# Holding ScalarE to the source's order while the first three QKV chunks are issued

## The chip, the cores and the metric

The kernel runs on one NeuronCore of a Trainium2 chip. The metric is the device time of one execution in microseconds (us). Below, PE is TensorE (matmuls), DVE is VectorE, ACT is ScalarE, POOL is GpSimd, and SP is SyncE, whose queue issues the large DMA loads. "Landing" of a load is the moment its data is in SBUF.

## The reference

A decoder trunk of two layers on 256 positions of width 2048, all in float32. Layer 0 has sliding-window attention (32 query heads, 4 key/value heads of 64), layer 1 a gated linear recurrence; each is followed by a squared-ReLU MLP of width 8192. Every half-layer is normalised and modulated by vectors computed from a conditioning vector. What matters here is the start of layer 0:

```python
cond = jax.nn.silu(c)
mod = cond @ mod_w[i] + mod_b[i]                       # 6 vectors of 2048 per layer
sh1, sc1, g1, sh2, sc2, g2 = jnp.split(mod, N_MOD, axis=-1)
h = modulate(rms_norm(x, norm_mix[i]), sh1, sc1)       # h * (1 + sc1) + sh1
proj = h @ w_in                                        # QKV: 2048 -> 2048 + 256 + 256
q = rms_norm(q, q_gain); k = rms_norm(k, k_gain)       # per head
out = softmax(banded q k^T with ALiBi and a sink) @ v
x = x + g1 * (out @ w_out)
h = modulate(rms_norm(x, norm_mlp[i]), sh2, sc2); a = relu(h @ w1); x = x + g2 * ((a * a) @ w2)
```

All weights are read once, 594 MB in all.

## The kernel before, in words

Weights come in pieces of 128 x 2048 float32 (1024 KB). A piece is loaded by SP into one of five `raw` buffers (`load_to`, L208 to L214). A weight piece then becomes two matmul operands: ACT rounds each half of it to `wh` (L250), DVE subtracts to get the remainder `wl` (L251). There are five half-size buffers for `wh` and five for `wl`, and a piece takes two of each. A product is three matmuls, weight-high times data-high, weight-high times data-low, and weight-low times data-high.

The pieces come in one list, `seq`, and are loaded in that order. In the QKV stage there are three kinds. "w" are weight pieces. "g" are modulation weights that PE multiplies with the conditioning vector straight from `raw` (`gemv`, 4 matmuls named `mm<-raw,cst`); after four of them a row is copied by ACT (L267), turned by PE (`gt`), and reduced by DVE into `mods` (L273). "m" are modulation weights that DVE multiplies and sums in one instruction (L233). A `raw` buffer is free again when its piece has been used: for w at the end of `wl`, for g at the end of the gemv, for m at the end of the DVE instruction.

The QKV product is split along its inner dimension into four chunks of 512 (chunk 0 to 3, the loop variable `s_`, L862), so that it can begin before all modulation vectors are known. A chunk has five w pieces (below w20 is the first piece of chunk 2), and each piece gives two results of 128 x 512 in PSUM, "halves" of the piece: 24 matmuls each. In chunks 0 to 2 a g and an m follow each of the first four pieces in `seq`, which makes 13 loads per chunk. ACT copies each half out of PSUM. In chunk 0 the copy goes straight to its place (`first_part`, L851, tiles `o`), in chunks 1 and 2 to a scratch tile `w` (`add_part`, L846) from which POOL adds it (L847). In chunk 3 DVE adds the last part, and what follows is the per-head normalisation: ACT squares (L676, L703), PE sums (`ssq`) and turns (`sst`), DVE takes the reciprocal root (L651, L132 to L138), widens it (L662), PE turns it back (`rbk`), DVE multiplies (L725), and the first attention pair (`S` matmuls) can begin. Before a chunk, its four input tiles `h` are made by DVE and ACT from `mods` (`make_h`: `ht` L547, `h` high part L551 on ACT, low part L552 on DVE).

In the source, `ahead(LAG - 1)` behind each piece's products prepares one piece more than the one that comes next: the `wh` casts of piece n+1 are written ahead of the products and copies of piece n.

The order in which each engine's instructions stand is not the source's. A scheduler in the recording layer (`TileContext`) orders them when the program is built. Instructions of one engine that don't depend on each other can change places. Two front ends hold PE to an order: `Queue` wraps an engine, remembers the name of its last instruction, and, where `pin` is true, adds to each new one a dependency on the one before, which costs no semaphore and no instruction. `pe` records without pinning, `pep` pins, and both share one `last`.

Of the kernel before, what the change touches and what calls it, by code (L numbers as in the profile page):

```python
# [41 lines left out]
class Queue:  # L42
# [5 lines left out]
    def __getattr__(self, name):  # L48
        fn = getattr(self.engine, name)

        def call(*args, **kw):
            r = fn(*args, **kw)  # L52
            if self.pin and self.last:
                self.tc.add_manual_dep(
                    r.ins, self.last[-1],
                    mybir.DependencyInfo(mybir.DependencyClass.NoSync, mybir.DependencyReason.DATA),
                    reason="issue order")
            self.last[:] = [r.ins.name]
            return r
        return call  # L60
# [2 lines left out]
@with_exitstack  # L63
def trunk(ctx, tc, a, out):
    nc = tc.nc
    dve, act, sp, pool_q = nc.vector, nc.scalar, nc.sync, nc.gpsimd
    last = []
    pe, pep = Queue(tc, nc.tensor, last, False), Queue(tc, nc.tensor, last, True)

# [239 lines left out]
    def ahead(extra, must=True):  # L309
        w = min(st["w"] + extra, len(wpos) - 1)  # L310
        while st["prep"] <= wpos[w]:
            if seq[st["prep"]][0] != "w" and st["hold"] and not must:
                break
            prep_one()
# [109 lines left out]
    def mm_quarter(op, k0, natural, evacs):  # L424
        key = st["w"]
        ahead(0)
        for j in range(2):
            ps = mmtile()
            wh, wl = W[key][j]
            if natural[j]:  # L430
                for k in range(4):
                    v_step(ps, wh, wl, k, op[k0 + k], k == 0, k == 3)
                    if k % 2 == 1:
                        hook()
            else:
                for u in range(2):
                    for k in range(4):
                        c = slice((4 * u + k) * P, (4 * u + k + 1) * P)
                        three(ps[:, u * T:(u + 1) * T], wh[:, c], wl[:, c], op[k0 + k], k == 0, k == 3)
                    hook()  # L440
            evacs[j](ps)
        W.pop(key)
        st["w"] += 1
        ahead(LAG - 1, False)
# [166 lines left out]
    with tc.tile_pool(name="attn", bufs=2) as ap:  # L611
# [207 lines left out]
        def step():  # L819
            s_ = steps[0]  # L820
            steps[0] += 1
            hook()
            if DT + DV <= s_ < 16 + DT + DV:
                pair_v(s_ - DT - DV)
            if DT <= s_ < 16 + DT:
                pair_t(s_ - DT)
            if s_ < 16:
                while s_ // 2 not in rq or not kdone:
                    hook()
                pair(s_)  # L830
            if 1 <= s_ < 17:
                pair_n(s_ - 1)
            if s_ >= 9:
                for _ in range(2):
                    if wo["k"] <= min(KB - 1, s_ - 5):
                        wo_step()
            hook()
            for _ in range(2):
                if seq[st["prep"]][0] != "w":
                    prep_one()  # L840
            ahead(0, False)
# [11 lines left out]
        def done_part(p):  # L853
# [6 lines left out]
                    evac_q(p - 2, ps, parts[p])  # L860
            return f
        for s_, fin_part in enumerate((first_part, add_part, add_part, done_part)):  # L862
            feed.need(4 * s_ + 4)
            st["hold"] = s_ == 3
            ahead(LAG - 1, False)
            for e in range(5):
                mm_quarter(H, 4 * s_, (False, e == 0), (fin_part(2 * e), fin_part(2 * e + 1)))
                feed.poll()
                for _ in range(SE if s_ == 3 and e > EE else 0):
                    step()  # L870
                ahead(LAG - 1, False)
# [483 lines left out]
```

## Time and profile before

| | us |
|---|---|
| three runs | 2344.27, 2355.24, 2355.31 |
| the profiled execution, its own time | 2348.51 |
| its span, first to last instruction | 2346.7 |
| PE busy | 2269.6 (97%) |
| DVE busy | 1788.2 (76%) |
| ACT busy | 1163.1 (50%) |
| POOL busy | 100.7 (4%) |

The profiled execution's time is 1.8 us more than its span. The page cuts the span into 40 slices of 58.7 us; PE is at nine tenths or more in all but the first five, which hold the start, the QKV stage and the attention. The mean granted TensorE clock is 0.99. In the tables below a row of a windows view has, for each stretch, its length, PE busy with the number of records, the granted clock, the busy share of the DMA engines and their GB/s (with all engines shown, PE, PEld, DVE, ACT, POOL come in that order). In a timeline a row is start, duration, engine, line, operation, tiles, and in brackets how long the engine had been idle and what ended that.

### The profile page before, as it was taken

The numbers are of one execution on the slowest core, as the hardware profiler recorded it, in microseconds if no ns is written. First come the engines' busy times: TensorE is split into PE (matmuls) and PEld (weight loads), VectorE is DVE, ScalarE is ACT, GpSimd is POOL, SyncE is SP. The second block draws the span as 40 slices with busy tenths as digits, with TensorE's granted clock in tenths as the row PEclk, the third lists the DMA queues.
The fourth block names the chain that finished last, engine by engine and source line by source line (L and its number), as shares of the span: only waits on it lengthen the run. The fifth ranks groups of instructions, "written<-read, shape, count | busy, mean of one in ns | idle before, by whom it ended". The sixth has DMA issues, their size and how long they took to land.

```text
span 2346.7 us, 37064 instructions
## 1 busy us (share of the span) xinstructions
PE 2269.6 (97%) x14690; PEld 1992.0 (85%) x14690; DVE 1788.2 (76%) x2908; ACT 1163.1 (50%) x1962; POOL 100.7 (4%) x94
## 2 busy tenths in 40 slices
PE   5887899999999999999999999999999999999999
PEld 3775579998888888888888898899888888888888
DVE  5668679975888898897998888767865766665665
ACT  3344454544444444455666666655544444444443
POOL 0133530000000000000000000000000000000000
PEclk8999999999999999999999999999999999999999
DMA  9886799756898899985577777645666666655552
GB/s 361 310 305 257 272 335 341 253 195 215 323 336 323 327 333 324 334 317 187 196 284 267 259 267 268 214 164 180 231 233 231 236 227 239 207 189 186 191 194 94
DMA packets 84638, 598.80 MB, mean 255 GB/s; under 512 B 9457, under 2 KB 11505, under 8 KB 12273
## 3 DMA queue, kind: packets, MB, share of 16 engines
q1 hardware_dynamic: 81936, 593.81, 70.3%
q8 instruction: 115, 1.88, 0.3%
q10 hardware_dynamic: 2304, 2.10, 0.3%
q0 software_dynamic: 224, 0.52, 0.1%
q14 instruction: 59, 0.48, 0.1%
HBM read 594.04 MB, written 2.10 MB: 254 GB/s over the span
## 4 chain that ended last, share of the span: by engine, by line
PE 92%; DVE 4%; ACT 2%; DMA 1%; issue 1%; POOL 0%; ACTq 0%; SPq 0%; DVEq 0%; POOLq 0%
PE mm L52 89%; ACT wh L250 1%; DVE raw L233 1%; PE A L52 1%; DVE wl L251 1%; PE on L52 0%; PE S L52 0%; POOL h L771 0%; DVE asm L751 0%; DMA raw<-in_aoutk_dram 0%; DMA raw<-in_mod_w_dram 0%; PE cb L52 0%; PE pt L52 0%; DVE h L552 0%; PE pv L52 0%
## 5 line engine op out<-in xcount | busy, mean ns | idle before, releaser
L251 DVE TENSOR_TENSOR wl<-raw,wh 128x1024 fp32r<-128x1024 f32 x744 | 909.3, 1226 | 429.7 <-ACT wh L250 427.9
L250 ACT CAST wh<-raw 128x1024 fp32r<-128x1024 f32 x744 | 778.4, 1050 | 850.9 <-PE mm L52 773.2
L52 PE MATMUL mm<-h,wh 128*128 128x512 f32 (+2 forms) x3728 | 1155.4, 368 | 35.1 <-ACT wh L250 34.6
L52 PE MATMUL mm<-h,wl 128*128 128x256 f32 (+1 forms) x3232 | 908.9, 282 | 1.5 <-DVE wl L251 1.4
L52 PE MATMUL mm<-o,wh 128*128 128x512 f32 (+2 forms) x3120 | 860.4, 346 | 0.2 <-ACT h L759 0.2
L52 PEld LDWEIGHTS mm<-h,wh 128*128 128x128 f32 x3728 | 671.5, 190 | 161.9 <-ACT wh L250 39.0
L52 PE MATMUL mm<-o,wl 128*128 128x256 f32 (+1 forms) x2432 | 679.2, 280 | 0.0
L52 PEld LDWEIGHTS mm<-h,wl 128*128 128x128 f32 x3232 | 612.2, 190 | 11.1 <-issue 3.4
L52 PEld LDWEIGHTS mm<-o,wh 128*128 128x128 f32 x3120 | 539.9, 189 | 82.3 <-issue 2.5
L52 PEld LDWEIGHTS mm<-o,wl 128*128 128x128 f32 x2432 | 457.9, 188 | 0.7 <-issue 0.3
L233 DVE CUSTOM_DVE_ANT_0 raw<-raw,cond 128x2048 f32<-128x2048 f32 x160 | 365.7, 2286 | 9.5 <-DMA raw<-in_mod_w_dram 9.3
L52 PE MATMUL mm<-wh,h 128*128 128x256 f32 x576 | 105.9, 283 | 4.2 <-DVE h L552 2.7
L52 PEld LDWEIGHTS mm<-wh,h 128*128 128x128 f32 x576 | 88.8, 188 | 8.0 <-DVE h L552 3.2
L52 PE MATMUL mm<-wl,h 128*128 128x256 f32 x288 | 81.0, 281 | 0.0
L472 ACT COPY w<-mm 128x256 f32<-128x256 f32 x186 | 68.1, 366 | 0.0
L771 POOL TENSOR_SCALAR h<-h,asm 128x128 f32<-128x128 f32 x64 | 64.6, 1027 | 69.7 <-DVE asm L754 21.1
L476 ACT CAST h<-w 128x256 fp32r<-128x256 f32 x125 | 49.8, 403 | 23.9 <-DVE w L967 23.0
L52 PEld LDWEIGHTS mm<-wl,h 128*128 128x128 f32 x288 | 54.3, 188 | 0.5 <-issue 0.4
L967 DVE SCALAR_TENSOR_TENSOR w<-w 128x256 f32<-128x256 f32 x125 | 52.0, 421 | 2.2
L477 DVE TENSOR_TENSOR h<-w,h 128x256 fp32r<-128x256 f32 x125 | 51.5, 417 | 0.0
L473 DVE TENSOR_TENSOR w<-mm,w 128x256 f32<-128x256 f32 x109 | 45.6, 418 | 0.4 <-ACT w L472 0.2
L988 DVE TENSOR_TENSOR acc<-mm,acc 128x256 f32<-128x256 f32 x96 | 40.5, 422 | 6.3 <-PE mm L52 3.8
(203 smaller groups left out, 1134.6 us busy)
## 6 DMA issues: line engine op xcount, KB each, us to landing
raw<-in_mod_w_dram SPq DMA_DIRECT2D x160, 1024.0 KB, 5.5
raw<-in_mlp_dram SPq DMA_DIRECT2D x128, 1024.0 KB, 4.9
raw<-in_hin_dram SPq DMA_DIRECT2D x64, 1024.0 KB, 5.0
raw<-in_mlp1b_dram SPq DMA_DIRECT2D x64, 1024.0 KB, 4.8
raw<-in_mlp1a_dram SPq DMA_DIRECT2D x48, 1024.0 KB, 5.2
raw<-in_mod_g_dram SPq DMA_DIRECT2D x32, 1024.0 KB, 6.1
raw<-in_ainq_dram SPq DMA_DIRECT2D x20, 1024.0 KB, 6.8
raw<-in_m1h_dram SPq DMA_DIRECT2D x16, 1024.0 KB, 5.1
```

Of the source, the lines that this page charges most:

```text
L52: r = fn(*args, **kw)
L233: dve.tensor_tensor_reduce(out=r, in0=r, in1=cond, scale=1.0, scalar=0.0, op0=ALU.mult, op1=ALU.add, accum_out=mods[:, e[1], e[2]:e[2] + 1])
L250: act.copy(out=wh, in_=part)
L251: dve.tensor_tensor(out=wl, in0=part, in1=wh.bitcast(F32), op=ALU.subtract)
L472: act.copy(out=t, in_=ps[:, T:])
L473: dve.tensor_tensor(out=out_t, in0=ps[:, :T], in1=t, op=ALU.add)
L476: act.copy(out=opt[:, :T], in_=src_t)
L477: dve.tensor_tensor(out=opt[:, T:2 * T], in0=src_t, in1=opt[:, :T].bitcast(F32), op=ALU.subtract)
L771: pool_q.tensor_scalar(out=Ls[hh][:, cut[b]], in0=Ls[hh][:, cut[b]], scalar1=ri[:, i:i + 1], scalar2=None, op0=ALU.mult)
L967: dve.scalar_tensor_tensor(out=t, in0=t, scalar=0.0, in1=t, op0=ALU.max, op1=ALU.mult)
L988: dve.tensor_tensor(out=acc[n], in0=ps[:, :T], in1=acc[n], op=ALU.add)
```

## The change

ACT gets a front end of its own (`act = Queue(tc, nc.scalar, [], False)`). It pins while the loop issues chunks 0 to 2 (`s_ < 3`), and not before or after. PE, DVE, POOL and SP are recorded as before. No instruction is added or taken away, and no buffer, size or wait is set by hand. The edit from `self.last` to `self.last[:1]` has the same truth value. Because all ACT calls now go through the wrapper, ACT's instructions bear the line L52 of the wrapper instead of their own, and the other lines behind L65 move by one, behind L863 by two.

```diff
         def call(*args, **kw):
             r = fn(*args, **kw)
-            if self.pin and self.last:
+            if self.pin and self.last[:1]:
                 self.tc.add_manual_dep(
...
     nc = tc.nc
-    dve, act, sp, pool_q = nc.vector, nc.scalar, nc.sync, nc.gpsimd
+    dve, sp, pool_q = nc.vector, nc.sync, nc.gpsimd
+    act = Queue(tc, nc.scalar, [], False)
     last = []
     pe, pep = Queue(tc, nc.tensor, last, False), Queue(tc, nc.tensor, last, True)
...
         for s_, fin_part in enumerate((first_part, add_part, add_part, done_part)):
+            act.pin = s_ < 3
             feed.need(4 * s_ + 4)
```

What it moves, in three places. First ACT in chunk 1. `raw_749` is w12, `raw_824` is w13; `mm_795` and `mm_833` are the two halves of w11, `mm_870` and `mm_908` those of w12. Before:

```order
L846 COPY w_783<-mm_758 128x512
L846 COPY w_830<-mm_795 128x512
L846 COPY w_858<-mm_833 128x512
L250 CAST wh_787<-raw_749 128x1024
L250 CAST wh_791<-raw_749 128x1024
L846 COPY w_905<-mm_870 128x512
L846 COPY w_933<-mm_908 128x512
L250 CAST wh_862<-raw_824 128x1024
```

Now:

```order
L52 COPY w_783<-mm_758 128x512
L52 CAST wh_787<-raw_749 128x1024
L52 CAST wh_791<-raw_749 128x1024
L52 COPY w_830<-mm_795 128x512
L52 COPY w_858<-mm_833 128x512
L52 CAST wh_862<-raw_824 128x1024
L52 CAST wh_866<-raw_824 128x1024
L52 COPY w_905<-mm_870 128x512
```

The casts of w12 stood behind both copies of w11 and now stand ahead of them, behind the last copy of w10; those of w13 likewise by one piece.

Second, DVE at the turn from chunk 1 to chunk 2. `raw_899` is w14, `raw_901` is w20, and `gt_1010` is the turned modulation row for chunk 2's `h8` to `h11`. Before:

```order
L273 TENSOR_REDUCE mods_81<-gt_1010 128x4
L531 TENSOR_TENSOR mods_81<-mods_81,cst_70 128x2 x2
L552 SCALAR_TENSOR_TENSOR h8_1034<-ht_1032,mods_81,h8_1034 128x256
L547 SCALAR_TENSOR_TENSOR ht_1045<-x2_75,gsc_139,rbs_218 128x256
L251 TENSOR_TENSOR wl_938<-raw_899,wh_937 128x1024
L251 TENSOR_TENSOR wl_942<-raw_899,wh_941 128x1024
L552 SCALAR_TENSOR_TENSOR h9_1039<-ht_1037,mods_81,h9_1039 128x256
L552 SCALAR_TENSOR_TENSOR h10_1047<-ht_1045,mods_81,h10_1047 128x256
L251 TENSOR_TENSOR wl_1020<-raw_901,wh_1019 128x1024
```

Now:

```order
L252 TENSOR_TENSOR wl_938<-raw_899,wh_937 128x1024
L252 TENSOR_TENSOR wl_942<-raw_899,wh_941 128x1024
L274 TENSOR_REDUCE mods_81<-gt_1010 128x4
L532 TENSOR_TENSOR mods_81<-mods_81,cst_70 128x2 x2
L252 TENSOR_TENSOR wl_1020<-raw_901,wh_1019 128x1024
L252 TENSOR_TENSOR wl_1024<-raw_901,wh_1023 128x1024
L553 SCALAR_TENSOR_TENSOR h8_1034<-ht_1032,mods_81,h8_1034 128x256
L553 SCALAR_TENSOR_TENSOR h9_1039<-ht_1037,mods_81,h9_1039 128x256
L548 SCALAR_TENSOR_TENSOR ht_1045<-x2_75,gsc_139,rbs_218 128x256
```

The remainders of w14 and w20 moved ahead of all of chunk 2's `h` low parts.

Third, PE where chunk 3's third piece, w32, ends (`mm_1737` is its second half) and the first pair begins. `sst_1713`, `rbk_1762` and `rbk_1771` belong to the normalisation of the first four query pairs, and `S_1784` is the first pair's score. Before:

```order
L52 MATMUL mm_1681<-h15_1453,wl_1601 128x256
L52 MATMUL sst_1713<-cst_70,w_1699 128x128 x2
L52 MATMUL mm_1737<-h12_1435,wh_1604 128x256 x2
...
L52 MATMUL mm_1737<-h15_1453,wl_1605 128x256
L52 MATMUL rbk_1762<-cst_70,w_1730 128x128 x4
L52 MATMUL rbk_1771<-cst_70,w_1732 128x128 x4
```

Now:

```order
L52 MATMUL mm_1737<-h15_1453,wh_1604 128x256 x2
L52 MATMUL mm_1737<-h15_1453,wl_1605 128x256
L52 MATMUL sst_1713<-cst_70,w_1699 128x128 x2
L52 MATMUL rbk_1762<-cst_70,w_1730 128x128 x4
L52 MATMUL rbk_1771<-cst_70,w_1732 128x128 x4
```

The 24 matmuls of w32's second half stood between `sst` and `rbk` and now stand ahead of both. From w33 on the order of ACT and PE is the same but for a few neighbours; DVE's differs in single places up to the fifth pair and is the same after that. SP's and POOL's rows are the same throughout.

## The prediction, made before the result was known

> **What bounds the kernel now.** I began with the page's first part and its slices.
>
> ```profile
> span 2346.7 us, 37064 instructions
> PE 2269.6 (97%) x14690; PEld 1992.0 (85%) x14690; DVE 1788.2 (76%) x2908; ACT 1163.1 (50%) x1962; POOL 100.7 (4%) x94
> PE   5887899999999999999999999999999999999999
> ```
>
> PE is the bound, 77 us of the span are without it, and the slices put nearly all of that into the first five (293 us). The change touches chunks 0 to 2 of QKV, so I next cut the start into stretches.
>
> ```profile
> core 0: us, PE busy (x) PEld busy (x) DVE busy (x) ACT busy (x) POOL busy (x), PEclk, DMA share, GB/s
> 57.20:81.00 23.80, 17.34 (x119) 14.29 (x118) 11.70 (x16) 9.70 (x14) 0.00 (x0) 0.93 0.89 333
> 81.00:125.60 44.60, 37.69 (x279) 31.86 (x279) 28.51 (x35) 18.40 (x28) 11.84 (x8) 0.96 0.84 310
> 125.60:170.20 44.60, 37.70 (x277) 31.87 (x277) 29.81 (x34) 17.56 (x27) 17.26 (x10) 0.96 0.84 308
> 340.00:400.00 60.00, 60.00 (x508) 60.00 (x507) 56.01 (x81) 27.64 (x48) 0.00 (x0) 1.00 0.90 337
> ```
>
> A chunk takes 44.6 us and no engine fills it; from 340 on PE fills everything. What does PE wait for? The groups of PE's instructions from 57 to 176 say it, idle time behind the second bar:
>
> ```profile
> L52 PE MATMUL mm<-h,wh 128*128 128x256 f32 x389 | 76.9, 296 | 19.8 <-ACT wh L250 19.7
> L52 PE MATMUL mm<-h,wl 128*128 128x256 f32 x194 | 57.6, 299 | 0.5 <-DVE wl L251 0.4
> ```
>
> All 20.3 us are waits for a weight piece to be split. Why is it split late? ACT's timeline and SP's issue of the same piece, w12, with that load's issue-to-landing time:
>
> ```profile
> 90.72 0.33 SPq L212 DMA_DIRECT2D raw<-in_ainq_dram  x1
> raw<-in_ainq_dram SPq DMA_DIRECT2D x1, 1024.0 KB, 4.9
> 96.77 0.59 ACT L846 COPY w<-mm 128x512 f32<-128x512 f32 x1 [2.46 <-PE mm L52]
> 100.62 0.59 ACT L846 COPY w<-mm 128x512 f32<-128x512 f32 x1 [3.27 <-PE mm L52]
> 101.10 2.00 ACT L250 CAST wh<-raw 128x1024 fp32r<-128x1024 f32 x2
> ```
>
> w12 had landed at 90.72 + 4.9 = 95.6. ACT idled 3.27 us before 100.62, with that piece lying there, because the copy of w11's second half stood ahead of it and waited for PE. So PE finishes w11, ACT copies, ACT casts, and PE waits meanwhile. The order on ACT sets the period.
>
> **The gaps have a second cost.** PE alone, one piece with its gemv per row; the first ran with no gap, the rest are w02, w03, w12, w13, w22, w23, each from the end of the piece before:
>
> ```profile
> 50.20:57.23 7.03, 7.03 (x58) 1.00 1.00 409
> 57.23:66.75 9.52, 7.46 (x56) 1.00 0.95 349
> 66.75:77.72 10.97, 8.91 (x58) 0.84 0.82 295
> 100.53:111.74 11.21, 9.09 (x56) 0.85 0.84 302
> 111.74:121.56 9.82, 7.67 (x59) 1.00 0.86 305
> 145.15:156.27 11.12, 9.01 (x56) 0.85 0.89 326
> 156.27:166.12 9.85, 7.71 (x59) 1.00 0.85 314
> ```
>
> The same 48 matmuls and gemv take 7.03 us unbroken, and up to 9.09 behind a gap of about 2.1, where the granted clock reads 0.84 or 0.85. [...] The rows have the slow clock in three gaps of six, and the measurement decides.
>
> **What the change does, part by part.** It adds and removes no instruction. (1) *The casts move ahead of the copies.* In chunks 0 to 2 the casts of piece n+1 now stand behind the last copy of piece n-1, hence run while PE is in piece n. The kernel before shows what that gives. In the chain of waits w04 is cast late (79.01), but the casts of w10 and w11 did lie ahead, and all three pieces then ran without a gap:
>
> ```profile
> 79.01 1.99 ACT wh L250 x2
> 81.04 19.50 PE mm L52 x158
> ```
>
> Removed are the gaps, 19.8 + 0.5 = 20.3, and the slow matmuls, (7.46 + 8.91 + 9.09 + 7.67 + 9.01 + 7.71) - 6 x 7.03 = 7.7. Together 28.0. A chunk would then take 4 x 7.03 + 6.0 (the fifth piece has no gemv: 7.03 less 1.06) + 0.6 for `gt` = 34.8.
>
> (2) *Can the loads follow?* 13 loads of 1.049 MB at the 409 GB/s of the first row above, where the DMA share is 1.00, take 33.3 us, less than 34.8. There is also a loop: SP may issue w(n+2) only when PE has consumed g(n).
>
> ```profile
> SPq L212 <- PE mm L52: 69.5, 21, 6.4
> 53.36 1.06 PE L52 MATMUL mm<-raw,cst 128*32 128x512 f32 x8
> DMA to landing us min/median/max: 4.7/6.5/9.1
> L251 DVE TENSOR_TENSOR wl<-raw,wh x744: 1205/1225/2042, 40.6 to 2329.7; 128x1024 fp32r<-128x1024 f32 x186
> ```
>
> In the piece that began at 50.2 the gemv ended 4.2 in. With the median landing of 6.5, a cast of 1.0 and a remainder of 1.2, the piece after next is ready 12.9 after the start, before the 14.1 of two pieces. With the longest landing it would be 15.5, a stall of 1.4. I take 0; the other end is 12 pieces x 1.4 = 17. Behind a cast that now waits for its landing stand the two copies of the piece in work. PE needs their PSUM buffers two pieces later (five buffers, two per piece), so a wait of 1 or 2 us there costs nothing; with the longest landing it is the same 1.4 per piece, already counted.
>
> (3) *The turn of a chunk.* DVE now makes both remainders first and then the next chunk's `h`. From the end of a chunk's fourth piece: copy 0.6, casts 2.0, last remainder 1.2, then four `h` low parts and two `ht`, six at about 0.44 (`ht` shows 0.88 for two, below): 6.5 us. PE has `gt` 0.6, the fifth piece 6.0, and nine matmuls (1.1) before it needs the last `h`: 7.7. It fits with 1.2 to spare, unless a POOL add (1.28) or two come between. Three turns, 0 to 4 us; I take 2.
>
> ```profile
> 38.26 0.88 DVE L547 SCALAR_TENSOR_TENSOR ht<-x,gsc,rbs 128x256 f32<-128x256 f32 x2
> ```
>
> (4) *The first query pairs in chunk 3.* The chain of waits before, and DVE there:
>
> ```profile
> 193.71 0.22 PE sst L52 x2
> 193.92 2.86 PE mm L52 x24
> 197.41 0.75 DVE L662 COPY w<-qw 128x512 f32<-128x512 f32 x2
> 198.08 2.28 DVE L233 CUSTOM_DVE_ANT_0 raw<-raw,cond 128x2048 f32<-128x2048 f32 x1
> 201.76 1.36 PE S L52 x7
> ```
>
> From `sst` to the first `S` are 201.76 - 193.92 = 7.8 us of DVE work (one m of 2.28 in it), and PE's last 24 matmuls covered 2.9. With those matmuls ahead of `sst` the cover is gone, and all behind waits 2.9 longer. I take 3. It is 0 if DVE is quicker there, since two of the additions it did meanwhile are then over, and 8 if the m in the chain also waits for its load. After that DVE's order differs in places, by the position of an m of 2.28 in a chain, up or down; I take 0, with 4 either way.
>
> Sum: 28.0 - 2 - 3 = 23.0 us. The profiled execution took 2348.5, the span plus 1.8, so 2325.5. The median of the three runs lies 6.7 above that execution and the lowest 4.2 below; all four average 2350.8. I predict **2326**.
>
> **The rivals.** *DVE and POOL in each other's way* (0.13). In chunks 1 and 2 POOL adds ten times, beside DVE. POOL's and DVE's timelines there:
>
> ```profile
> 94.38 2.85 POOL L847 TENSOR_TENSOR o<-o,w 128x512 f32<-128x512 f32 x1 [2.71 <-ACT w L846]
> 97.43 1.28 POOL L847 TENSOR_TENSOR o<-o,w 128x512 f32<-128x512 f32 x1 [0.20 <-ACT w L846]
> 93.81 2.28 DVE L233 CUSTOM_DVE_ANT_0 raw<-raw,cond 128x2048 f32<-128x2048 f32 x1
> 96.13 1.12 DVE L531 TENSOR_TENSOR mods<-mods,cst 128x2 f32<-128x2 f32 x1
> 97.28 0.16 DVE L539 SCALAR_TENSOR_TENSOR gsc<-mods,cst 128x2 f32<-128x2 f32 x1
> ```
>
> The add took 2.85 instead of 1.28 and ended 1.2 behind the DVE sum; DVE's tiny addition behind it took 1.12 where its like takes 0.16. They look as if they took turns. If so in full, a chunk needs DVE's 28.5 of 81 to 125.6, less two remainders it has over (2.5), plus ten adds (12.8), 38.8 us against 34.8: 4.0 more in each of two chunks, **2334**. [...] Against it stands that DVE can run a piece ahead of PE, and some of its instructions ran beside an add at their usual length.
>
> *Landings late* (0.06). The loop of (2) takes the longest landing each time: 17 given back, **2343**. For it: both loads and copies crowd when the period shrinks. Against it: 9.1 was the second of two loads issued at once.
>
> *The attention takes it back* (0.07). If the loads of 180 to 330 set that stage's end whatever the start, all 23 are lost, **2348**. It has 48 loads by SP's timeline, 123 us at 409 GB/s, in a stretch of 150, so it has room; each of them waits for a buffer, and the freeing of that moves along.
>
> *The transfers are the bound already* (0.04). If 310 GB/s is what these mixed loads can reach, and not what the waiting let through, the casts wait for landings instead of copies, the chunk stays at 44.6, and (3) and (4) are paid for nothing: 2348.5 + 2 + 3, **2353**, slower than before. It decides as soon as a load needs 3.4 us (44.6 / 13); 409 GB/s with PE busy all the while speaks against it, and so do the 5.5 us that w12 lay in SBUF. That the change does nothing is excluded by the order rows.
>
> **How the numbers follow.** The forecast has 0.70. Low end: 2325.5 without the 5 of (3) and (4), with 4 from DVE's order and a run as fast as the lowest: 2313, rounded. High end: the forecast with (3) at 4, (4) at 8 and the first rival's 8, plus a few us of the runs' spread: 2342. A measurement of this kernel can tell about 0.5% from no change, 11.8 us, so faster means below 2343.5. Faster: 0.70 + 0.13 + half of 0.06 = 0.86; same 0.12; slower 0.02.
>
> **What would show it.** PE's waits for `wh` from 57 on gone, chunk 1 and 2 near 35 us with clock 1.00 and DMA share above 0.95; the first `S` at about 176 instead of 201.8; the stage from 330 on only shifted. I am wrong if PE waits there for `wl` (DVE and POOL) or the casts for DMA; if chunks shorten but `S` or the end don't follow, the loss is in (4) or behind.

## The result, and the profile after

| | before | after |
|---|---|---|
| median of 4 runs each, same chip | 2352.56 | 2325.04 (2320.82 to 2325.91) |
| the profiled execution, its own time | 2348.51 | 2325.76 |
| its span | 2346.7 | 2324.0 |

The ratio is 0.9885, 95% interval 0.9856 to 0.9915: faster by about 1.15%. In two experiments below, raw4 and prepdve, one execution was slow throughout (2487.76 and 4542.81 us); their times are medians of the others. The page's first part and PE's slices:

```profile
span 2324.0 us, 37074 instructions
...
PE 2265.4 (97%) x14690; PEld 1988.7 (86%) x14690; DVE 1792.2 (77%) x2908; ACT 1161.4 (50%) x1962; POOL 107.8 (5%) x94
...
PE   5998899999999999999999999999999999999999
```

The page counts 37074 instructions, 10 more than before, although the edit adds none. The counts of the five busy rows are the same, so the ten are among the instructions that are not counted as busy.

The windows of the start, the first up to chunk 1, the next two inside chunks 1 and 2, then the head of the attention (columns as in the prediction's windows, all engines):

```profile
57.00:81.00 24.00, 24.00 (x192) 20.96 (x191) 16.65 (x22) 13.00 (x20) 0.00 (x0) 1.00 1.00 407
81.00:116.00 35.00, 34.57 (x273) 29.39 (x272) 28.43 (x34) 16.66 (x25) 14.88 (x9) 1.00 0.98 389
116.00:151.00 35.00, 34.42 (x273) 29.70 (x271) 32.05 (x33) 15.94 (x24) 20.77 (x10) 1.00 0.96 379
151.00:186.00 35.00, 28.30 (x210) 21.89 (x214) 28.27 (x70) 13.65 (x28) 4.65 (x6) 0.90 0.62 222
186.00:220.00 34.00, 25.97 (x187) 17.05 (x180) 27.49 (x84) 15.72 (x56) 24.30 (x20) 0.90 0.74 279
```

PE is full to 151 at clock 1.00, and the transfers run at 0.96 to 1.00 of their time. From 151 to 220 PE stands still 14.7 us. PE's groups from 57 to 150 have lost the waits for `wh`, and a matmul takes 284 ns instead of 296:

```profile
L52 PE MATMUL mm<-h,wh 128*128 128x256 f32 x393 | 72.1, 284 | 0.6 <-ACT h L52 0.4
L52 PE MATMUL mm<-h,wl 128*128 128x256 f32 x197 | 55.6, 285 | 0.0
```

What waits now is ACT, for landings (its waits from 57 to 150, then those of before from 57 to 176):

```profile
ACT wh L52 <- DMA raw<-in_ainq_dram: 20.0, 7, 4.4
ACT w L52 <- PE mm L52: 15.2, 8, 3.4
```

```profile
ACT w L846 <- PE mm L52: 40.6, 16, 4.9
ACT o L851 <- PE mm L52: 17.6, 7, 4.7
```

The casts left the copies' shadow and follow the loads instead. They are a piece ahead, so PE sees nothing of it.

### The profile page after: what moved, and what is told of

It reads as the page before. It is cut to its first block, busy times and chain, and to the rows that moved or that the text cites. A ratio compares the mean times of both kernels' runs of the same rounds, so it can differ in the third digit from the quotient of the medians.

```text
span 2324.0 us, 37074 instructions
## 1 busy us (share of the span) xinstructions
PE 2265.4 (97%) x14690; PEld 1988.7 (86%) x14690; DVE 1792.2 (77%) x2908; ACT 1161.4 (50%) x1962; POOL 107.8 (5%) x94
## 4 chain that ended last, share of the span: by engine, by line
PE 93%; DVE 4%; DMA 2%; ACT 1%; issue 1%; POOL 0%; DVEq 0%; ACTq 0%
PE mm L52 88%; DVE wl L252 1%; DVE raw L234 1%; PE A L52 1%; DMA raw<-in_mod_w_dram 1%; PE S L52 1%; PE on L52 0%; PE pt L52 0%; ACT wh L52 0%; PE pv L52 0%; DMA raw<-in_aoutk_dram 0%; DMA raw<-in_ainq_dram 0%; ACT h L52 0%; PE rbk L52 0%; PE cb L52 0%
## 5 line engine op out<-in xcount | busy, mean ns | idle before, releaser
L52 ACT CAST wh<-raw 128x1024 fp32r<-128x1024 f32 x744 | 778.1, 1051 | 877.5 <-PE mm L52 768.0
L52 PE MATMUL mm<-h,wh 128*128 128x512 f32 (+2 forms) x3728 | 1150.7, 367 | 15.6 <-ACT wh L52 14.5
L52 PE MATMUL mm<-h,wl 128*128 128x256 f32 (+1 forms) x3232 | 906.4, 281 | 1.0 <-DVE wl L252 1.0
L52 PE MATMUL mm<-o,wh 128*128 128x512 f32 (+2 forms) x3120 | 859.0, 346 | 1.2 <-ACT o L52 0.9
L52 PEld LDWEIGHTS mm<-h,wh 128*128 128x128 f32 x3728 | 668.7, 189 | 143.2 <-ACT wh L52 15.3
L52 PE MATMUL mm<-o,wl 128*128 128x256 f32 (+1 forms) x2432 | 678.5, 280 | 0.0
L52 PEld LDWEIGHTS mm<-h,wl 128*128 128x128 f32 x3232 | 610.4, 189 | 8.2 <-issue 5.4
L52 PEld LDWEIGHTS mm<-o,wh 128*128 128x128 f32 x3120 | 538.7, 188 | 82.9 <-issue 2.2
L52 PEld LDWEIGHTS mm<-o,wl 128*128 128x128 f32 x2432 | 457.2, 188 | 0.7 <-issue 0.3
L234 DVE CUSTOM_DVE_ANT_0 raw<-raw,cond 128x2048 f32<-128x2048 f32 x160 | 368.9, 2306 | 25.5 <-DMA raw<-in_mod_w_dram 25.2
L52 ACT COPY w<-mm 128x256 f32<-128x256 f32 (+1 forms) x308 | 118.2, 386 | 24.0 <-PE mm L52 24.0
L52 PE MATMUL mm<-wh,h 128*128 128x256 f32 x576 | 106.8, 285 | 4.2 <-DVE h L553 2.7
L52 PEld LDWEIGHTS mm<-wh,h 128*128 128x128 f32 x576 | 89.8, 190 | 7.8 <-DVE h L553 3.2
L52 PE MATMUL mm<-wl,h 128*128 128x256 f32 x288 | 81.4, 283 | 0.0
L52 ACT CAST h<-w 128x256 fp32r<-128x256 f32 x125 | 49.8, 403 | 27.5 <-DVE w L969 26.7
L52 PEld LDWEIGHTS mm<-wl,h 128*128 128x128 f32 x288 | 54.7, 190 | 0.2
```

Of the source, the lines that this page charges most:

```text
L234: dve.tensor_tensor_reduce(out=r, in0=r, in1=cond, scale=1.0, scalar=0.0, op0=ALU.mult, op1=ALU.add, accum_out=mods[:, e[1], e[2]:e[2] + 1])
```

## The experiments

Times are medians. There were four sets of runs, each with its own runs of the kernel before (medians 2349.7, 2350.8, 2349.8, 2348.9), and ratios are to those. Lengths of chunk 1 and chunk 2 are those of windows cut at the first `gt` of each chunk: 43.83 and 44.57 before, 34.71 and 36.12 in the change.

**Pinned, but with late casts** (late):

```diff
             W[e[1]] = []
-            for i in range(2):
+            def split():                    # casts and remainders as they were
...
+            if st["late"]:                  # chunks 0 to 2
+                held.append(run)            # split, then the raw buffer is free
+            else:
+                split()
...
             evacs[j](ps)
+        while held:                         # behind both copies of a piece
+            held.pop(0)()
```

> ACT is pinned while chunks 0 to 2 are issued, as in the change, but the source's order itself is altered: the two casts of a piece are written behind both copies of the piece before it, which is about the order of the kernel before. Theory (the place of the casts sets the period): PE waits for wh about 20 us again in the three chunks, chunk 1 takes about 44 to 46 us, the first S is near 200, the time is 2343 to 2360, so no gain. Rival (the gain comes from the pinning itself or from what else the scheduler moved): about 2325, chunk 1 near 35 us.

Measured: 2360.37, ratio 1.004 (1.0026 to 1.0054), just above the range expected; chunks 45.23 and 46.12; first `S` at 212.3, where I had expected about 200. Its PE group from 57 to 176:

```profile
L52 PE MATMUL mm<-h,wh 128*128 128x256 f32 x370 | 74.3, 298 | 19.6 <-ACT wh L52 19.6
```

The pin alone gains nothing. The place of the casts is the gain: with them behind the copies (and with them the remainders and the release of the `raw` buffer) the 19.6 us and the 298 ns are back. The kernel is not the one before in all respects: from the first `gt` of chunk 3 to the first `S` it takes 42.8 us, against 35.7 before, and I did not trace why. The comparison rests on chunks 1 and 2.

**The gaps filled** (late-fill), the same kernel with 16 matmuls behind each piece whose result nobody reads:

```diff
+                if s_ < 3:
...
+                    for _ in range(16):
+                        pep.matmul(warm, lhsT=identb, rhs=distb[:, :T], start=True, stop=True)
```

> As the run with late casts, with 16 matmuls of 128x256 in bf16 on constant tiles put on PE behind each piece of chunks 0 to 2, whose result nobody reads. They need no weight piece, so they run while PE would wait; at about 0.12 us each they fill 1.9 us of a gap of about 2.2. Theory (an idle gap of 2 us costs a slow clock afterwards): the clock reads 1.00 through the chunks, the matmuls behind the gap take 7.0 to 7.4 us instead of up to 9.1, and the time is about 8 us (5 to 11) below the run without them, although PE does more. Rival (a gap of 2 us has no such cost, or the slow clock has another cause): clock still 0.84 behind the gaps, time equal to the run without them or a few us above.

Measured: 2354.76, ratio 1.0019 (1.0003 to 1.0034), 5.6 us below the run without the matmuls. PE's groups, same window:

```profile
L52 PE MATMUL mm<-h,wh 128*128 128x256 f32 x376 | 71.1, 287 | 1.4 <-ACT wh L52 1.3
...
L52 PE MATMUL warm<-distb,identb 128*128 128x256 bf16 x208 | 24.9, 273 | 0.0
```

The matmuls of the pieces are 11 ns shorter and the clock from 76 to 170 reads 1.00 instead of 0.98: where the gaps are filled, the slow clock is gone. Not every gap brought it. In chunk 1 of the run without the filling PE waited 7.1 us for `wh`, and the clock read 1.00:

```profile
78.22:123.45 45.23, 38.05 (x278) 30.59 (x277) 26.70 (x33) 17.42 (x25) 8.99 (x7) 1.00 0.79 301
```

The time is only partly a test, since the added matmuls take 9.6 us per chunk, more than the waits they fill (6.7 to 7.1): the first `gt` of chunk 3 comes at 169.99, without them at 169.57. The first `S` comes 2.3 us earlier (210.0 against 212.3). The rest of the 5.6 us appears behind it, and I did not trace where.

**One chunk alone** (chunk1): `act.pin = s_ == 1`.

> ACT is pinned in chunk 1 alone (s_ == 1). Chunks 0 and 2 and the head of chunk 3 have the order of the kernel before. Theory: one chunk gains a third of 28 us, less the turn behind it (0 to 2), and nothing is lost at the head of chunk 3: chunk 1 takes 35 to 36 us, the chunks beside it 43 to 45, the time is 7 to 9.5 us below the kernel before, 2341 to 2345 where that is 2350. Rival (pace set elsewhere, given back in the next chunk since loads or DVE are late): the following chunk is longer by what this one gains, time as before.

Measured: 2342.59, ratio 0.9961 (0.9946 to 0.9976), so 7.1 us by the medians and 9.2 by the ratio. First `S` at 192.69, 9.0 earlier than before. Chunks 1 and 2 take 37.24 and 41.18 us, where I had expected 35 to 36 and 43 to 45; together they are 10.0 shorter than before. That is about a third of the gain, and none of it is taken back in the chunk behind.

**POOL and DVE** (add2, noadd), a second addition behind each one, or none:

```diff
                 pool_q.tensor_tensor(out=parts[p], in0=parts[p], in1=t, op=ALU.add)
+                pool_q.tensor_tensor(out=spare, in0=parts[p], in1=parts[p], op=ALU.add)
```

> The change, with a second addition on POOL behind each addition of chunks 1 and 2, into a tile that nobody reads. This puts to the test the rival by which DVE and POOL are in each other's way. In the change DVE is busy 32.1 us of the 35 from 116 to 151, with the waiting beside POOL in it, and PE does not wait for it. Rival's mechanism (DVE and POOL take turns): 10 more additions per chunk cost DVE about 1.1 to 1.3 us each, 43 to 45 us of DVE per chunk, so it becomes the bound, PE waits for wl, chunks 1 and 2 take 43 to 45 us instead of 35, and the time is 14 to 20 us above the change, near 2340. Without it (the additions run beside DVE): chunks within 1 us of 35, time within 3 us of the change.

> The change without POOL's additions in chunks 1 and 2 (so the parts of chunks 1 and 2 are left out of the sum, and the values behind are not the reference's; all else runs as before). If DVE and POOL take turns but DVE has room left: DVE's busy time from 116 to 151 falls from 32.1 to 22 to 27 us, its remainders take 1.2 us each again, and chunks and time stay within 2 us of the change. If the additions do bind the change's chunks in part: chunks 0.5 us or more shorter and the time 1 to 4 us lower.

Measured: 2336.06 with twice the additions, ratio 0.9937 (0.9914 to 0.996); 2324.36 with none, ratio 0.9882 (0.9861 to 0.9904). Chunks 1 and 2 of the change, of the doubled and of the bare run (PE, PEld, DVE, ACT, POOL, clock, DMA):

```profile
72.40:107.11 34.71, 34.71 (x278) 29.84 (x277) 27.60 (x34) 17.55 (x27) 11.01 (x6) 1.00 0.98 391
107.11:143.23 36.12, 35.67 (x278) 30.28 (x277) 33.07 (x34) 17.07 (x26) 21.83 (x10) 1.00 0.96 378
```

```profile
72.44:109.66 37.22, 35.43 (x279) 30.12 (x278) 33.86 (x34) 18.99 (x29) 21.96 (x13) 1.00 0.97 380
109.66:152.40 42.74, 37.69 (x278) 30.82 (x277) 42.35 (x34) 18.14 (x26) 38.59 (x20) 0.96 0.86 325
```

```profile
71.67:106.38 34.71, 34.71 (x279) 29.84 (x277) 25.57 (x34) 17.73 (x27) 0.00 (x0) 1.00 1.00 395
106.38:142.03 35.65, 35.22 (x278) 30.11 (x277) 24.86 (x34) 16.77 (x25) 0.00 (x0) 1.00 0.99 393
```

The doubled run is 11 us slower than the change, where the rival's mechanism in full would have made it 14 to 20. DVE's 34 instructions of chunk 2 take 24.86, 33.07 and 42.35 us with 0, 10 and 20 additions, 0.8 to 0.9 for each. So the two are in each other's way, and DVE's time decides where it reaches the chunk's, as in the doubled run (42.35 of 42.74). The change lies 3 us below that point (33.07 of 36.12). Without the additions its time is the same within the noise. In the doubled run PE waits for `wl` (its waits from 57 to 153):

```profile
PE mm L52 <- DVE wl L252: 5.0, 5, 1.5
```

**Four raw buffers** (raw4): `NRAW = 4` instead of 5.

> The change with four raw buffers instead of five. This puts the loop of step 2 (load, cast, product, next load) to the test, and the rival of late landings. In the change most casts start within 0.1 us of their landing, so the loads have no room over. Theory (the loop of 12.9 of 14.1 us has little room, and one buffer less takes it): casts wait for DMA, DMA share in the chunks falls below 0.9, chunks take 37 to 42 us, the time is 8 to 25 us above the change, part of it in the later stages that use the same buffers. Rival (there is room in the loop): chunks 35 to 36 us, the time within 3 us of the change.

Measured: 2332.09, ratio 0.9918 (0.9891 to 0.9945), some 7 us above the change, a little less than the 8 to 25 expected; the two intervals overlap. ACT's and PE's waits from 57 to 151:

```profile
ACT wh L52 <- DMA raw<-in_ainq_dram: 40.0, 9, 6.3
```

```profile
PE mm L52 <- ACT wh L52: 4.9, 8, 1.2
```

Chunks 37.80 and 39.70, the DMA share 0.92 to 0.94 (I expected below 0.9). The chunks and the waits decide here more than the time: with five buffers the loads are just early enough for PE, with four the wait for landings doubles and reaches it.

**The head of chunk 3.** PE held as well (pe3), DVE held (dve3):

```diff
+                pe.pin = s_ == 3                          # pe3
                 mm_quarter(H, 4 * s_, ...)
+                pe.pin = False
...
+    dve = Queue(tc, nc.vector, [], False)                 # dve3
             act.pin = s_ < 3
+            dve.pin = s_ == 3                             # all of chunk 3, attention steps too
```

> The change, and PE held to the source's order in chunk 3 as well, which puts 24 matmuls of w32 behind sst of the first query pairs again, as they stood before. Theory (step 4: this order of PE costs the head of chunk 3 some 3 to 5 us): the first S comes 3 to 5 us earlier than with the change alone (near 176 instead of 180.6), and the time is 3 to 5 us lower than the change's, about 2321, ratio to before 0.987 where the change has 0.9885. Rival (the chain waits for something else, such as the load of w33 or the m sums): first S within 1 us of 180.6 and the time within 1 us of the change's.

> The change, and DVE held to the source's order while chunk 3 is issued. The chain from sst to the widened factors then has no m sum and no remainder in it (in the change an m of 2.28 stands in it, in the run with PE held, remainders of 2.44). Theory (what is lost at the head of chunk 3 is DVE's order, not PE's): sst to rbk falls from 5.5 to about 3.5 us, the first S comes 2 to 4 us earlier than in the change (177 to 179). If nothing behind takes it back the time is 2 to 4 us lower than the change's, ratio near 0.987. Rival (the m sums that now come later hold raw buffers, the loads behind them start later, and the attention stage gives it back): first S earlier, but the time equal to the change's or a few us above.

Then the modulation pieces used earlier, with DVE held (dve3m), not held (prep), or held only to the first attention step (prepdve):

```diff
                 feed.poll()
+                if s_ == 3 and e < 2:
+                    for _ in range(2):
+                        if seq[st["prep"]][0] != "w":
+                            prep_one()
                 for _ in range(SE if s_ == 3 and e > EE else 0):
                     step()
+                    dve.pin = False                       # prepdve
```

> The change itself once more, so that the runs beside it have it on the same chip. Theory and rivals alike: ratio 0.986 to 0.992, near 2324, first S near 180.6.

> The run with DVE held to the source's order in chunk 3, and the source altered: two loaded modulation pieces (a g and an m) are used behind each of the first two weight pieces of chunk 3, instead of waiting for the attention steps. DVE then has an m before each of the two chains and none within them, so the raw buffers come free as early as in the change. Theory (with DVE held alone the loss came from raw buffers held by late m sums): DMA share from 151 to 186 back from 0.41 to 0.6 or more, first S at 175 to 179 (in the change 180.6), the time 2 to 6 us below the change's, ratio 0.985 to 0.988. Rival (the loss came from the remainders of w33 and w34 standing late in DVE's fixed order, or from PE waiting there): DMA share recovers, but the time stays 5 us or more above the change's.

> The change with the same alteration of the source in chunk 3, but DVE left to the scheduler. An m still stands in the chain from sst to rbk. Theory (the chain's length is set by what DVE does within it): sst to rbk stays at 5 to 6 us, the first S is at 180 to 183, the time within 3 us of the change's. Rival (the earlier use of the modulation pieces is what helps, not DVE's order): the time falls as much as in the run where DVE is held as well.

> The run in which two modulation pieces are used behind each of the first two pieces of chunk 3, and DVE held to the source's order from the start of chunk 3 to the first attention step behind w32, no longer (the two runs with DVE held kept it through all of chunk 3, the attention steps between its pieces included). Theory (holding DVE through the attention steps is what cost 11 to 15 us there, the clean chain in itself gains): first S near 177 instead of 180.8, the time 2 to 4 us below the run with the modulation pieces alone (2322), so 2318 to 2320, ratio 0.986 to 0.987. Rival (a first S that comes earlier is worth nothing, because PE waits for a later chain until DVE has caught up): first S near 177, the time at 2321 to 2326, and more idle time of PE from 186 to 220.

| | first `S` at | DMA share 151 to 186 | time | ratio to before |
|---|---|---|---|---|
| change | 180.56 | 0.62 | 2325.04 | 0.9885 (0.9856 to 0.9915) |
| change again | 180.82 | 0.63 | 2325.88 | 0.9901 (0.9884 to 0.9918) |
| pe3 | 182.94 | 0.62 | 2327.18 | 0.9895 (0.9876 to 0.9913) |
| dve3 | 175.29 | 0.41 | 2337.01 | 0.9939 (0.9920 to 0.9958) |
| dve3m | 177.33 | 0.73 | 2340.40 | 0.9958 (0.9943 to 0.9973) |
| prep | 180.84 | 0.85 | 2322.00 | 0.9879 (0.9862 to 0.9897) |
| prepdve | 179.08 | 0.70 | 2327.51 | 0.9904 (0.9884 to 0.9924) |

Putting the 24 matmuls back behind `sst` is not enough by itself: in pe3 the first `S` comes later than in the change, where I had expected it 3 to 5 us earlier. The run does not single out PE's order, though. Held in order, PE now waits twice in chunk 3 ahead of that `sst`:

```profile
156.97 0.62 PE L52 MATMUL ssq<-w,cst 128*32 128x256 f32 x4 [2.87 <-ACT w L52]
...
163.98 0.63 PE L52 MATMUL rbk<-cst,w 128*128 128x128 f32 x4 [2.89 <-DVE w L663]
```

And the scheduler put other work of DVE into the chain. DVE in the change, then in pe3 (some rows of the chain from `qw<-sst` to the widening copy):

```profile
172.40 0.23 DVE L652 SCALAR_TENSOR_TENSOR qw<-sst,cst 128x8 f32<-128x8 f32 x2
...
173.38 2.28 DVE L234 CUSTOM_DVE_ANT_0 raw<-raw,cond 128x2048 f32<-128x2048 f32 x1
...
176.91 0.76 DVE L663 COPY w<-qw 128x512 f32<-128x512 f32 x2
177.59 1.22 DVE L252 TENSOR_TENSOR wl<-raw,wh 128x1024 fp32r<-128x1024 f32 x1
```

```profile
172.87 0.24 DVE L652 SCALAR_TENSOR_TENSOR qw<-sst,cst 128x8 f32<-128x8 f32 x2 [1.08 <-PE sst L52]
...
176.41 1.22 DVE L252 TENSOR_TENSOR wl<-raw,wh 128x1024 fp32r<-128x1024 f32 x1
...
177.63 1.22 DVE L252 TENSOR_TENSOR wl<-raw,wh 128x1024 fp32r<-128x1024 f32 x1
...
179.39 0.76 DVE L663 COPY w<-qw 128x512 f32<-128x512 f32 x2
```

The chain is 4.5 us with the m in it, 6.5 with two remainders and a wait for PE. Held to the source (dve3) it is 2.4 and `S` comes 5.3 us earlier, yet the kernel is 11 to 12 us slower. In this run `sst` also stands ahead of the last 17 matmuls of w32, so the 5.3 us are not DVE's order alone. Its chain:

```profile
168.94 0.24 DVE L52 SCALAR_TENSOR_TENSOR qw<-sst,cst 128x8 f32<-128x8 f32 x2 [3.71 <-PE sst L52]
...
171.37 0.76 DVE L52 COPY w<-qw 128x512 f32<-128x512 f32 x2
```

My first reason for the loss, m sums that hold raw buffers, fits the DMA share of 0.41 but not the time: with the m sums early (dve3m) the share is 0.73 and the time no better. PE's waits in dve3m from 150 to 330, and in the change:

```profile
PE pt L52 <- POOL h L773: 6.9, 4, 3.3
PE ssq L52 <- ACT w L52: 5.6, 5, 2.5
PE pv L52 <- DVE o L52: 5.1, 2, 3.1
PE rbk L52 <- DVE w L52: 2.8, 3, 2.1
```

```profile
PE rbk L52 <- DVE w L663: 18.4, 5, 6.5
PE ssq L52 <- ACT w L52: 1.7, 2, 0.9
```

The waits for the chain fell from 18.4 to 2.8, and the three others of dve3m add up to 17.6. None of them is for a weight piece (in dve3 waits for `wh` and `wl` were 9.1), so late remainders of w33 and w34, the rival, are not what PE waits for there. But all of PE's waits in this window differ by only 2 us (24.9 against 23.0), while the last `pv` comes at 321.9 instead of 307.2. The granted clock is lower as well, 0.92 against 0.94 over the three windows from 151 on, to 186, 220 and 330 (0.97, 0.85 and 0.92, in the change 0.90, 0.90 and 0.97), an estimate of 5 us. What makes up the rest is not shown.

Releasing DVE at the first attention step (prepdve against dve3m) gives back 12.9 us, so holding it from that step on was the cost. But a clean first chain still gains nothing: `S` is 1.8 earlier than in prep, and the time 5.5 higher where I had expected 2 to 4 lower (the intervals of the two overlap). The run without additions says the same: its first `S` comes at 177.03, 3.5 earlier than in the change, and its time is only 0.7 lower. In prep itself the transfers go on (0.85) and PE's waits for the chain fall to 13.6. At 2322.00 (2319.03 to 2322.38) against 2325.88 (2322.34 to 2331.61) beside it, prep has the lowest median of all, though here too the intervals of the ratios overlap.

## Why the prediction was right

The sum was 2325.5 for the profiled execution, which took 2325.76; the median predicted was 2326, measured 2325.04. The steps are borne out, but an agreement within 1 us is luck: single executions of the kernel before, in the same set, lie between 2344.27 and 2355.31, the medians differ by 27.5 us here and by 23.9 in the repeat, and some terms erred in opposite directions. By its steps:

(1) *Casts ahead of the copies: 28.0 predicted.* PE from its first matmul of chunk 0 to its last of w32, cut at the first `gt` of each chunk, is 156.11 us before (40.67 to 196.78) and 130.89 in the change (41.09 to 171.98). The sums of the two windows views:

```profile
sum 156.11, PE 134.39; mean PE 33.60
```

```profile
sum 130.89, PE 128.34; mean PE 32.09
```

PE's idle time fell from 21.72 to 2.55, by 19.2 where 20.3 was predicted. Its busy time for the same work fell by 6.0, where 7.7 was predicted for the slow matmuls. Most of that is the clock: before it read 0.89, 0.96, 0.96 and 1.00 in the four windows, in the change 0.92 and then 1.00, which by an estimate (length times what is missing to 1.00) is 5.1 us. The clock does not explain the rest; in the prediction's own rows the pieces with 1.00 also took 0.4 to 0.7 longer than the unbroken one. The slow clock itself is shown by the runs (0.84 to 0.85 in three of the prediction's six rows with gaps, and 1.00 from 57 to 151 in the change, where PE's waits for `wh` are gone); why the other three, with gaps of the same 2.1 us, read 1.00 was not shown.

(2) *The loads can follow: 0.* Right for PE, but barely, as raw4 shows. A chunk was foretold at 34.8 (its terms add up to 34.7); chunks 1 and 2 took 34.71 and 36.12. The prediction named casts that wait for DMA as a sign of being wrong. That sign came, 20.0 us of it, and was the wrong one to watch: the casts stayed a piece ahead, and of PE's waits from 57 to 150 none is for `wh` (the only one is 0.4 us, for `h`).

(3) *Three turns: 2.* To the end of w32's matmuls the gain is 156.11 - 130.89 = 25.2; steps 1 and 3 together had 26.0. At two turns PE waited 0.43 and 0.44 for `h`. So the turns cost less than predicted, and step 1 gave less.

(4) *The head of chunk 3: 3.* From there to the first `S` 3.7 were lost (the last matmul of w32 came 196.78 - 171.98 = 24.8 us earlier, the first `S` 21.1). PE before, then in the change:

```profile
193.54 0.38 PE L52 MATMUL sst<-cst,w 128*128 128x128 f32 x2
...
197.98 1.06 PE L52 MATMUL rbk<-cst,w 128*128 128x128 f32 x8 [1.21 <-DVE w L662]
201.12 0.64 PE L52 MATMUL ssq<-w,cst 128*32 128x256 f32 x8 [2.08 <-DVE o L725]
201.69 0.50 PE L52 MATMUL S<-distb,identb 128*128 128x384 bf16 x2
```

```profile
171.59 0.38 PE L52 MATMUL sst<-cst,w 128*128 128x128 f32 x2
177.49 1.94 PE L52 MATMUL rbk<-cst,w 128*128 128x128 f32 x8 [5.52 <-DVE w L663]
179.55 1.08 PE L52 MATMUL ssq<-w,cst 128*32 128x256 f32 x8
180.56 0.82 PE L52 MATMUL S<-distb,identb 128*128 128x384 bf16 x2
```

Before, w32's matmuls ran on for 3.2 us behind the start of `sst`; in the change for 0.4. That is 2.9 of the 3.7, the cover whose loss the prediction had priced. The other 0.8 is a longer way from `sst` to `S` (8.97 against 8.15). In it stands the m, now ahead of `rbk` and not behind it, and a cost that the prediction left out: in the 5.5 us wait and behind it the granted clock reads 0.50 (176.0 to 180.5; before, from 197.0 to 201.5, 1.00), and the eight `rbk` take 1.94 instead of 1.06. This is read from the traces; neither pe3 nor dve3 separates PE's cover from DVE's order. The sign foretold, first `S` at about 176, left out the prediction's own term of 3; with it 179, measured 180.56. Behind the first `S` 1.6 came back, within the 0 with 4 either way.

*The rivals.* DVE and POOL: they were in each other's way, at a lower price than the rival had put on it. My 28.5 of DVE already held its waits beside POOL, and an addition cost DVE 0.8 to 0.9, not 1.28: 24.9 + 10 x 0.82 = 33, which fits into 36. If DVE had stood still for the whole of each addition, the estimate for its time in the doubled run's chunk 2 would be 24.9 + 20 x 1.28 = 50; it was 42.35, in a chunk of 42.74. How the two hold each other up was not shown, only what an addition cost. The attention took nothing back, and the transfers did not hold the chunks at 44.6: they moved 378 to 407 GB/s.

## What to carry to other kernels

When a copy out and a preparation stand in one engine's order, ask which of the two the matmul engine needs first; here the preparation stood behind a copy that waited for that engine (3.27 us of it with w12 already landed). Price such a serial wait with the slow clock behind it (here 0.84 to 0.85 in three pieces of six), and count what the removed wait had hidden: DVE had 3 us of a chunk left afterwards, the loads less. The gap that the change itself opened at the head of chunk 3 brought the slow clock too (0.50 from 176.0 to 180.5). An earlier start of a later chain is worth nothing unless the whole stage follows; here two runs with the first `S` 1.8 and 3.5 us earlier were not clearly faster. Holding one more engine to the source's order cost 11 to 15 us where the scheduler had been interleaving steps.

## What was not expected

An addition on POOL lengthened DVE's work in chunk 2 by about two thirds of its own 1.28 us (0.8 to 0.9). On average `wl` takes 1222 ns without additions and 1547 beside them, a 128x2 addition 160 and 600 (means from 81 to 151, bare run and change):

```profile
L252 DVE TENSOR_TENSOR wl<-raw,wh 128x1024 fp32r<-128x1024 f32 x21 | 24.8, 1222 | 9.3 <-ACT wh L52 9.3
...
L532 DVE TENSOR_TENSOR mods<-mods,cst 128x2 f32<-128x2 f32 x8 | 1.1, 160 | 0.2
```

```profile
L252 DVE TENSOR_TENSOR wl<-raw,wh 128x1024 fp32r<-128x1024 f32 x20 | 30.1, 1547 | 2.9 <-ACT wh L52 2.9
...
L532 DVE TENSOR_TENSOR mods<-mods,cst 128x2 f32<-128x2 f32 x8 | 4.6, 600 | 0.2
```
